# Score products from stacked q parts and doubled k parts, in both mixers of an encoder trunk

## The chip, the core and the metric

The kernel runs on one core of a Trainium2 chip. The metric is the device time of one execution in microseconds. Several executions of one program are timed, and their median is compared. One execution is also profiled: a trace of the instructions of each engine and of the DMAs, and a page that sums it up. The engines are called PE (matrix products; PEld is its loading of the stationary operand), DVE (vector), ACT (scalar and activation), POOL (general purpose, and one of the issuers of DMAs) and SP (issuer of DMAs).

## The reference

Two requests, 512 and 256 tokens of width 1024, go through a trunk of two layers with shared weights. Each layer is a half-weighted SwiGLU, a mixer, and another half-weighted SwiGLU. The first mixer has a gated part and a windowed attention with 8 query heads on 2 key heads; the second is a neighbourhood attention with 16 heads on a grid 64 wide. Only the scores matter for the change, and in both mixers they are a product over the 64 elements of a head:

```python
# first mixer (windowed attention, HEAD_DIM = 64)
s = jnp.einsum('bnqgrd,bnkgd->bngrqk', qb, kw).astype(jnp.float32) * (HEAD_DIM ** -0.5)
...
# second mixer (neighbourhood attention)
s = jnp.einsum('bchd,bacjhd->bhcaj', q_row, k_win).astype(jnp.float32) * (HEAD_DIM ** -0.5)
```

All is float32 in the reference. After the scores come a bias or mask, a softmax and a product with the values.

## The kernel before

**Parts.** Activations lie with the features on the 128 partitions and the tokens (512 of the prompt, then 256 of the sample, 768 in all) along the free dimension. PE multiplies operands of type float32r. To keep accuracy, each operand is split into a high part (a rounding cast on ACT) and a low part (the rest, a subtraction on DVE). A product of two split operands is then the sum of three products: high with high, high with low, low with high. `mm3` (L235) does this for the projections.

**Scores.** A projection of 128 output features gives two heads: head 0 in partitions 0 to 63 and head 1 in 64 to 127. `parts2` splits such a block of q or k for both heads at once, with the factor −1/8 for q. `halves3` makes the scores of both heads for one block of 128 queries: three products, and for each of them one matmul per head, whose operands are 64 partitions high. So a block takes six matmuls of half height, the two heads alternating. Their results go to PSUM banks of the pool `aux`, which has four.

**First mixer (`mixer0`).** k is projected once, for both key heads, and v with it. Then come four projections of q (`q_heads`), each for two of the eight query heads; q tiles have four buffers. `attention` runs as a chain beside the other projections: `score` for a pair of q projections and a block of queries, `turn` (transposes of the probabilities and their split) and `values`.

**Second mixer (`mixer1`).** Eight pairs of heads follow each other. `qk(pr)` loads the weights and projects q and k of a pair, for the prompt columns first and then for the sample columns, four projections; DVE scales each result by the row norm into a tile `qk`. The prompt tokens are kept turned: tile columns are shifted by 64 against the token order, and to have blocks of queries that wrap around, the tile is 64 columns longer (`TE`), with its first 64 columns copied to its end (L1709). The chain `parts(pr)` then splits them into the tiles of q and k, appends the pair to `heads`, and ends. The q and k tiles have one buffer each, so `parts(pr)` waits until the scores of the pair before are placed. The chain `attention` takes the pairs in order: while there is no new pair in `heads` it looks again every 0.5; then it places `scores(pr, 0)` and `scores(pr, 1)` (prompt, two blocks of queries each) and `scores(pr, 2)` (sample, two blocks), with the transposes and value products of the pair before in between. `bias` makes the additive terms for the next pair on POOL.

**What sets the order.** PE executes its instructions in the order in which the Python code emits them. The other engines' order is chosen by a scheduler from the dependencies. The emission is a hand-made interleaving: `self.t` is a clock that advances with each emitted matmul by an estimate (`mmul`: columns/2400, at least 0.107, in us). Chains are generators that yield a delay and are stepped by `tick` after every `mm3` when the clock has reached their time. `run_until` and `drain` step chains without emitting anything else, and set the clock forward to each chain's time while doing so. In `mixer1` this is the loop over quads of heads:

```python
for qd in range(4):
    for i in (0, 1):
        if last:
            self.drain(last)
        new = qk(2 * qd + i)
        ...
        last = self.spawn(parts(2 * qd + i, new, vt, 2 * i))
        if i == 0:
            v_heads(qd, vt)
```

So `parts` of an even pair runs beside the projections of v (`v_heads`), and `parts` of an odd pair is drained at once, before the next pair's `qk`, or, for the last pair, before the output projection.

Of the kernel before, what the change touches and what calls it, by code (L numbers as in the profile page):

```python
# [10 lines left out]
F32 = mybir.dt.float32  # L11
F32R = mybir.dt.float32r
# [40 lines left out]
class Trunk:  # L53
# [1051 lines left out]
    def norm_r(self, mp, cols):  # L1105
# [4 lines left out]
        if cols:  # L1110
            acc = mp.tile([P, T], F32, tag="accp", name="accp")
            for a, b, to in self.turned():
                nc.scalar.copy(acc[:, to : to + b - a], self.acc[:, a:b])
            yield 1.0
# [115 lines left out]
    def halves3(self, ps, st, mv):  # L1230

        for i, (a, b) in enumerate(((0, 0), (0, 1), (1, 0))):
            for h in (0, 1):
                self.mmul(ps[h], st[h][a], mv[h][b], i == 0, i == 2)
# [14 lines left out]
    def mixer0(self):  # L1249
# [54 lines left out]
        kh = mp.tile([P, T], F32R, tag="kh", name="kh")  # L1304
        kl = mp.tile([P, T], F32R, tag="kl", name="kl")
# [13 lines left out]
        for g in (0, 1):  # L1319
            c0, c1 = GROUPS[g]  # L1320
            t = roped(pkv[g][0], c0, c1)
            self.parts2(kh[:, c0:c1], kl[:, c0:c1], t)
# [8 lines left out]
        def q_heads(m):  # L1331
            q = [mp.tile([P, T], F32R, tag=f"q{n}", name=f"q{n}", bufs=4) for n in "hl"]
            w = self.unit("l0_w_in", 0, KD, 1024 + m * P, P)
            for g in (0, 1):
                c0, c1 = GROUPS[g]
                t = roped(self.proj(w, xs, GROUPS[g]), c0, c1)
                self.parts2(q[0][:, c0:c1], q[1][:, c0:c1], t, -0.125)
            qheads.append(q)

        def score(rp, n):  # L1340
# [4 lines left out]
            rows = lambda h: slice(h * 64, h * 64 + 64)  # L1345
            mv = [(kh[rows(h), cols], kl[rows(h), cols]) for h in (0, 1)]
# [6 lines left out]
            for r in (0, 1):  # L1353
# [4 lines left out]
                q = qheads[2 * rp + r]  # L1358
                self.halves3(dst, [tuple(t[rows(h), n * P : (n + 1) * P] for t in q) for h in (0, 1)], mv)
# [155 lines left out]
    def mixer1(self):  # L1515
# [6 lines left out]
        TE = TA + 64  # L1522
# [25 lines left out]
        SCORE = [(128 * j + 64, 128 * j + 64 * (j == 0), 128 * j + 256 - 64 * (j == 3), 64 * (j == 0)) for j in range(4)]  # L1548
        SCORE += [(TE + P * j, TE + 96 * j, TE + 96 * j + 160, 96 * j) for j in range(2)]
# [10 lines left out]
        def scores(pr, s):  # L1560
# [3 lines left out]
            for i in (0, 1):  # L1564
# [5 lines left out]
                rows = lambda h: slice(h * 64, h * 64 + 64)  # L1570
                self.halves3(
                    dst, [tuple(t[rows(h), qc : qc + P] for t in q) for h in (0, 1)],
                    [tuple(t[rows(h), c0:c1] for t in k) for h in (0, 1)],
                )
# [109 lines left out]
        def parts(pr, t, vt, hv):  # L1684
# [4 lines left out]
            q, k = ([mp.tile([P, TE + TB], F32R, tag=f"{n}{i}", name=f"{n}{i}") for i in "hl"] for n in "qk")  # L1689
            st = mp.tile([P, 4, 16], F32, tag="st", name="st", bufs=2)  # L1690
            for g, (c0, c1) in enumerate(((0, TE), (TE, TE + TB))):
                for which, d in ((0, q), (1, k)):
# [257 lines left out]
```

## Time and profile before

| | |
|---|---|
| median of 3 runs | 2551.85 us (2550.28 to 2552.0) |
| profiled execution, its own time | 2551.05 us |
| its span, first to last instruction | 2549.3 us |
| mean granted PE clock | 0.998 |
| first score product of the first mixer | at 540.1 us of the span |
| score products of the second mixer | begin from 1731.6 to 1984.4 us of the span |

The span is shorter than the execution's time by what lies before the first and after the last instruction. Busy times are unions of the instructions' durations. Matmuls overlap in the pipeline, so the time that one takes from the engine is read from one start to the next and not from its duration. A group of instructions is named by its line, engine, operation and tiles as output<-inputs; the products of one helper all bear the helper's line, L192, and are told apart by their tiles: `kh`, `kl`, `qh` and `ql` are the high and low parts of k and q before. The granted clock is the share of full speed that PE's throttle let through.

### The profile page before, as it was taken

How to read it: one execution, taken by the hardware profiler on the slowest of the kernel's cores; microseconds unless marked ns; L12 is line 12 of the kernel's file. 1: busy time of each engine (PE TensorE's matmuls, PEld its weight loads, DVE VectorE, ACT ScalarE, POOL GpSimd, SP SyncE). 2: the span in 40 equal slices, each digit the busy share in tenths (PEclk: the TensorE clock that was granted, in tenths of full speed). 3: DMA queues.
4: the chain of work that ended last, by engine and by line, in shares of the span. 5: the costliest groups of instructions: out<-in, count | busy, mean ns of one | idle time of the engine just before them, and what ended most of it. 6: DMA issues, size and time to landing. Idle time of an engine off the chain costs nothing.

```text
span 2549.3 us, 42552 instructions
## 1 busy us (share of the span) xinstructions
PE 2532.7 (99%) x15160; PEld 2460.6 (97%) x15160; DVE 2092.9 (82%) x4199; ACT 1369.1 (54%) x2843; POOL 323.3 (13%) x398
## 2 busy tenths in 40 slices
PE   9999999999999999999999999999999999999998
PEld 9999999988899999999999999998999899999998
DVE  8987888888879778788988888886667598878887
ACT  7544455556665545445655445554555475444553
POOL 1110110000111111110111011112112111101100
PEclk9999999999999999999999999999999999999999
DMA  8654555431256445552665455532222256545541
GB/s 238 159 132 121 131 134 147 147 96 61 77 140 177 115 130 125 131 130 82 155 154 133 119 128 125 120 127 69 65 61 77 76 150 168 131 119 125 124 125 53
DMA packets 187156, 310.88 MB, mean 122 GB/s; under 512 B 31680, under 2 KB 46528, under 8 KB 186944
## 3 DMA queue, kind: packets, MB, share of 16 engines
q1 hardware_dynamic: 149248, 240.49, 29.3%
q0 software_dynamic: 36864, 67.13, 16.7%
q8 instruction: 119, 1.95, 0.3%
q14 instruction: 93, 0.76, 0.1%
q10 hardware_dynamic: 832, 0.55, 0.1%
HBM read 298.65 MB, written 15.07 MB: 123 GB/s over the span
## 4 chain that ended last, share of the span: by engine, by line
PE 92%; DVE 4%; ACT 1%; issue 1%; DMA 1%; POOL 0%; SPq 0%; ACTq 0%; DVEq 0%; POOLq 0%
PE ps_mm L192 60%; PE ps_aux L192 30%; PE ps_aux L203 1%; DVE wlo L169 1%; DMA s<-in_w 1%; DMA raw<-in_w 0%; DVE u L588 0%; DVE s L746 0%; ACT whi L168 0%; DVE tl L256 0%; ACT p L1217 0%; ACT ug L1493 0%; DMA x<-in_x 0%; DVE db L256 0%; DVE o L1402 0%
## 5 line engine op out<-in xcount | busy, mean ns | idle before, releaser
L168 ACT CAST whi<-s 128x512 fp32r<-128x512 f32 x508 | 310.6, 620 | 384.2 <-PE ps_mm L192 199.1
L169 DVE TENSOR_TENSOR wlo<-s,whi 128x512 fp32r<-128x512 f32 x508 | 344.8, 686 | 173.6 <-ACT whi L168 152.4
L149 POOL DMA_DIRECT2D s<-in_w x256 | 223.8, 917 | 1439.9 <-DVE db L256 376.4
L168 ACT CAST whi<-rawp 128x512 fp32r<-128x512 f32 x344 | 211.5, 619 | 255.1 <-issue 100.0
L169 DVE TENSOR_TENSOR wlo<-rawp,whi 128x512 fp32r<-128x512 f32 x344 | 234.0, 685 | 23.2 <-ACT whi L168 14.2
L192 PE MATMUL ps_mm<-db,whi 128*128 128x384 f32 (+1 forms) x948 | 240.2, 334 | 0.0
L192 PE MATMUL ps_aux<-dt,whi 128*128 128x384 f32 x880 | 223.3, 334 | 0.0
L192 PEld LDWEIGHTS ps_mm<-db,whi 128*128 128x128 f32 x948 | 170.9, 188 | 0.0
L192 PE MATMUL ps_mm<-db,wlo 128*128 128x384 f32 (+1 forms) x474 | 158.3, 334 | 0.8 <-DVE wlo L169 0.8
L192 PEld LDWEIGHTS ps_aux<-dt,whi 128*128 128x128 f32 x880 | 158.9, 188 | 0.0
L192 PE MATMUL ps_aux<-dt,wlo 128*128 128x384 f32 x440 | 147.2, 334 | 0.4 <-DVE wlo L169 0.3
L168 ACT CAST whi<-raw 128x512 fp32r<-128x512 f32 x164 | 100.4, 619 | 67.8 <-PE ps_mm L192 44.3
L169 DVE TENSOR_TENSOR wlo<-raw,whi 128x512 fp32r<-128x512 f32 x146 | 99.0, 687 | 20.8 <-ACT whi L168 19.8
L588 DVE TENSOR_TENSOR u<-ps_aux,u 128x384 f32<-128x384 f32 x176 | 97.0, 551 | 7.6 <-PE ps_aux L192 7.6
L1217 ACT ACTIVATE p<-p,st 128x256 f32<-128x256 f32 (+3 forms) x144 | 69.1, 481 | 50.5 <-DVE st L1212 50.4
L192 PEld LDWEIGHTS ps_mm<-db,wlo 128*128 128x128 f32 x474 | 89.0, 188 | 1.4 <-DVE wlo L169 1.4
L582 ACT COPY u<-ps_mm 128x384 f32<-128x384 f32 x176 | 83.4, 474 | 1.9 <-PE ps_mm L192 1.6
L192 PEld LDWEIGHTS ps_aux<-dt,wlo 128*128 128x128 f32 x440 | 82.6, 188 | 1.0 <-DVE wlo L169 1.0
L746 DVE TENSOR_TENSOR s<-s,rawp 128x512 f32<-128x512 f32 x120 | 81.8, 687 | 2.0
L598 ACT ACTIVATE u<-u 128x384 f32<-128x384 f32 x88 | 46.2, 525 | 67.2 <-DVE u L597 67.1
L746 DVE TENSOR_TENSOR s<-rawp,s 128x512 f32<-128x512 f32 x120 | 81.8, 682 | 0.1
L192 PE MATMUL ps_aux<-dn,whi 128*128 128x384 f32 x320 | 81.2, 334 | 0.0
(772 smaller groups left out, 8231.2 us busy)
## 6 DMA issues: line engine op xcount, KB each, us to landing
rawp<-in_w SPq DMA_DIRECT2D x384, 256.0 KB, 3.1
s<-in_w SPq DMA_DIRECT2D x256, 256.0 KB, 2.8
s<-in_w POOLq DMA_DIRECT2D x256, 256.0 KB, 4.9
raw<-in_w SPq DMA_DIRECT2D x163, 256.0 KB, 2.8
xdm<-x SPq DMA_DIRECT2D x16, 384.0 KB, 2.3
x<-in_x SPq DMA_DIRECT2D x16, 192.0 KB, 4.5
x<-xdm SPq DMA_DIRECT2D x8, 384.0 KB, 4.9
tab<-skew SPq DMA_DIRECT2D x8, 256.0 KB, 3.7
```

The costliest lines, as they stand in the source:

```text
L149: self.nc.gpsimd.dma_start(f, y, accum_op=ALU.add)
L168: i = nc.scalar.copy(hi, src).ins
L169: self.behind = i, (eng or nc.gpsimd).tensor_tensor(out=lo, in0=src, in1=hi.bitcast(F32), op=ALU.subtract).ins
L192: self.nc.tensor.matmul(out, lhsT=lhsT, rhs=rhs, start=start, stop=stop, **kw)
L203: self.nc.tensor.transpose(out, src, self.ident)
L582: nc.scalar.copy(e[n, out], bank[key, n])
L588: nc.vector.tensor_tensor(out=t, in0=bank[key, n], in1=t, op=ALU.add)
L598: nc.scalar.activation(t, t, AF.Silu, scale=-1.0 if i else 1.0)
L746: f = lambda o, x, y: self.nc.vector.tensor_tensor(out=o, in0=x, in1=y, op=ALU.add)
L1217: nc.scalar.activation(outs[i - n0], outs[i - n0], AF.Exp, scale=-1.0, bias=mn[:, i : i + 1], accum_out=sm[:, i : i + 1])
```

## The change

Both mixers store the parts of q and k in another way, so that one product over 128 partitions covers two of the part products.

- **q stacked** (`stacked`). There is one q tile per head. In the head's own 64 partitions lies the high part, and in the other 64 the low part. Each is written by an op on 64 partitions (ACT for the high part, DVE for the low part).
- **k in both row halves** (`twice`). There are, per head, a tile (or half of a tile) with the high part of k in both row halves, and one with its low part in both.
- **Two products per head** (`stacks`). q stacked times k high twice, and times k low twice, both of full height: (high + low) · high + (high + low) · low. Low with low, which was left out before, is now in the sum. A block of queries takes four matmuls instead of six.
- **First mixer.** `twice` writes both row halves on ACT and DVE: four ops of 64 partitions on each, where there was one of 128. q tiles have three buffers instead of four.
- **Second mixer.** `twice` writes the head's own half only (`both=False`), k before q, and when both column groups are written, a DMA issued by POOL for each head copies the parts to the other half: 64 partitions of 2 × 768 elements. A delay of 2.0 on the emission clock is added before the pair is appended to `heads`.
- **No wrap copy.** The scaling into `qk` now writes the prompt columns in turned order, in two ops, so the copy of L1709 and the 64 extra columns are gone, and the blocks of queries start at multiples of 128.
- The turned copy of the norm's sums takes the tile `k0` instead of one of its own.

```diff
+    def stacks(self, ps, st, mv):
+        for h in (0, 1):
+            for i in (0, 1):
+                self.mmul(ps[h], st[h], mv[h][i], i == 0, i == 1)
+
+    def stacked(self, out, src, h, scale):
+        a, b = (slice(i * 64, i * 64 + 64) for i in (h, 1 - h))
+        self.nc.scalar.activation(out[a], src[a], AF.Copy, scale=scale)
+        self.nc.vector.scalar_tensor_tensor(
+            out=out[b], in0=src[a], scalar=scale, in1=out[a].bitcast(F32), op0=ALU.mult, op1=ALU.subtract
+        )
+
+    def twice(self, hi, lo, src, h, both=True):
+        a, b = (slice(i * 64, i * 64 + 64) for i in (h, 1 - h))
+        for r in (a, b) if both else (a,):
+            self.nc.scalar.copy(hi[r], src[a])
+        for r in (a, b) if both else (a,):
+            self.nc.vector.tensor_tensor(out=lo[r], in0=src[a], in1=hi[a].bitcast(F32), op=ALU.subtract)
...
@@ first mixer
-        kh = mp.tile([P, T], F32R, tag="kh", name="kh")
-        kl = mp.tile([P, T], F32R, tag="kl", name="kl")
+        ks = [[mp.tile([P, T], F32R, tag=f"k{n}{h}", name=f"k{n}{h}") for n in "hl"] for h in (0, 1)]
...
-            self.parts2(kh[:, c0:c1], kl[:, c0:c1], t)
+            for h in (0, 1):
+                self.twice(*(u[:, c0:c1] for u in ks[h]), t, h)
...
-            q = [mp.tile([P, T], F32R, tag=f"q{n}", name=f"q{n}", bufs=4) for n in "hl"]
+            q = [mp.tile([P, T], F32R, tag=f"q{h}", name=f"q{h}", bufs=3) for h in (0, 1)]
...
-                self.parts2(q[0][:, c0:c1], q[1][:, c0:c1], t, -0.125)
+                for h in (0, 1):
+                    self.stacked(q[h][:, c0:c1], t, h, -0.125)
...
@@ second mixer, parts
-            q, k = ([mp.tile([P, TE + TB], F32R, tag=f"{n}{i}", name=f"{n}{i}") for i in "hl"] for n in "qk")
+            q = [mp.tile([P, T], F32R, tag=f"q{h}", name=f"q{h}") for h in (0, 1)]
+            k = [mp.tile([P, 2, T], F32R, tag=f"k{h}", name=f"k{h}") for h in (0, 1)]
             st = mp.tile([P, 4, 16], F32, tag="st", name="st", bufs=2)
-            for g, (c0, c1) in enumerate(((0, TE), (TE, TE + TB))):
-                for which, d in ((0, q), (1, k)):
-                    self.parts2(d[0][:, c0:c1], d[1][:, c0:c1], t[g, which], None if which else -0.125)
+            for which in (1, 0):
+                for g, (c0, c1) in enumerate(GROUPS):
+                    for h in (0, 1):
+                        if which:
+                            self.twice(*(k[h][:, i, c0:c1] for i in (0, 1)), t[g, 1], h, False)
+                        else:
+                            self.stacked(q[h][:, c0:c1], t[g, 0], h, -0.125)
                     yield 0.3
+                for h in (0, 1) if which else ():
+                    a, b = (slice(i * 64, i * 64 + 64) for i in (h, 1 - h))
+                    nc.gpsimd.dma_start(k[h][b], k[h][a])
+            yield 2.0
             heads.append((q, k, st, vt, hv))
...
@@ second mixer, qk
-                    res[g, which] = t = mp.tile([P, n if g else TE], F32, tag=f"qk{g}", name=f"qk{g}", bufs=2)
-                    nc.vector.tensor_tensor(out=t[:, :n], in0=ps[:, :n], in1=self.rt[:, t0:t1], op=ALU.mult)
-                    if g == 0:
-                        nc.vector.tensor_copy(t[:, TA:TE], t[:, 0 : TE - TA])
+                    res[g, which] = t = mp.tile([P, n], F32, tag=f"qk{g}", name=f"qk{g}", bufs=2)
+                    for a, b, to in ((0, n, 0),) if g else ((64, TA, 0), (0, 64, TA - 64)):
+                        nc.vector.tensor_tensor(
+                            out=t[:, to : to + b - a], in0=ps[:, a:b], in1=self.rt[:, t0 + a : t0 + b], op=ALU.mult
+                        )
```

In both mixers the calls of `halves3` become calls of `stacks`, with a whole q tile of each head as stationary operand and the two k parts of that head as moving ones.

More of the change, by code (lines that the diff above doesn't have):

```diff
@@ L1110, in norm_r @@
         if cols:
-            acc = mp.tile([P, T], F32, tag="accp", name="accp")
+            acc = mp.tile([P, 2, T], F32, tag="k0", name="accp")[:, 0, :]
             for a, b, to in self.turned():
@@ L1228, in finish_rows @@
             )
[L1230 to L1234, printed above, removed]
+    def stacks(self, ps, st, mv):
[14 more added lines that the diff above has]
+            self.nc.vector.tensor_tensor(out=lo[r], in0=src[a], in1=hi[a].bitcast(F32), op=ALU.subtract)
     def parts2(self, hi, lo, src, scale=None):
@@ L1344, in score @@
             cols = slice(blks[0] * P, (blks[-1] + 1) * P)
-            rows = lambda h: slice(h * 64, h * 64 + 64)
-            mv = [(kh[rows(h), cols], kl[rows(h), cols]) for h in (0, 1)]
+            mv = [[t[:, cols] for t in k] for k in ks]
             m0 = (blks[0] - n + 1) * P
@@ L1357, in score @@
                 dst = [t[:, o : o + nk * P] for t in ps]
-                q = qheads[2 * rp + r]
-                self.halves3(dst, [tuple(t[rows(h), n * P : (n + 1) * P] for t in q) for h in (0, 1)], mv)
+                self.stacks(dst, [t[:, n * P : (n + 1) * P] for t in qheads[2 * rp + r]], mv)
                 todo += dst
@@ L1521, in mixer1 @@
         self.xcols = lambda k, c0, c1: tuple(self.cut(t[k], c0, c1) for t in xs)
-        TE = TA + 64
         mb = mp.tile([P, NMASK], BF16, tag="mb", name="mb")
@@ L1546, in mixer1 @@
         ot = {}
-        SCORE = [(128 * j + 64, 128 * j + 64 * (j == 0), 128 * j + 256 - 64 * (j == 3), 64 * (j == 0)) for j in range(4)]
-        SCORE += [(TE + P * j, TE + 96 * j, TE + 96 * j + 160, 96 * j) for j in range(2)]
+        SCORE = [(P * j, max(P * j - 64, 0), min(P * j + 192, TA), 64 * (j == 0)) for j in range(4)]
+        SCORE += [(TA + P * j, TA + 96 * j, TA + 96 * j + 160, 96 * j) for j in range(2)]
         pp = {}
@@ L1569, in scores @@
                 dst = [t[:, o : o + n] for t in ps]
[L1570 to L1574, printed above, removed]
+                self.stacks(dst, [t[:, qc : qc + P] for t in q], [[t[:, i, c0:c1] for i in (0, 1)] for t in k])
                 ps_list += dst
```

## The prediction

> **What bounds the kernel now.** I read the page's engine shares first, then the chain that ended last, then the busy time by stretch for the two mixers, and last the timeline around the score products.
>
> ```profile
> span 2549.3 us, 42552 instructions
> PE   2532.7 (99%) x15160; PEld 2460.6 (97%) x15160; DVE 2092.9 (82%) x4199; ACT 1369.1 (54%) x2843; POOL 323.3 (13%) x398
> PE 92%; DVE 4%; ACT 1%; issue 1%; DMA 1%; POOL 0%; SPq 0%; ACTq 0%; DVEq 0%; POOLq 0%
> ...
> 500.00:680.00 180.00, 177.96 (x1102) 152.56 (x1101) 151.37 (x415) 110.60 (x231) 9.25 (x8) 0.99 0.27 85
> 1720.00:2000.00 280.00, 279.97 (x2061) 253.80 (x2061) 193.11 (x554) 148.15 (x389) 58.31 (x82) 1.00 0.22 70
> ```
>
> In the last two rows the columns are stretch, length, and busy time of PE, PEld, DVE, ACT and POOL. PE is the bound. In the second mixer's score stretch (1720 to 2000) it was busy 279.97 of 280 us, so each PE step saved there is time saved, and each new PE wait is time lost. In the first mixer (500 to 680) it stood 2.0 us, and DVE was 84% busy.
>
> **Removed: half-height score products.** A timeline row is start, duration, engine, line, output<-inputs, shape.
>
> ```profile
> 1800.72 0.28 PE L192 MATMUL ps_mm<-wlo,xh3a 128*128 128x256 f32 x1
> 1800.84 0.28 PE L192 MATMUL ps_mm<-whi,xl3a 128*128 128x256 f32 x1
> 1801.05 0.39 PE L192 MATMUL ps_aux<-kh,qh 64*128 64x256 f32 x2
> 1801.27 0.28 PE L192 MATMUL ps_aux<-kl,qh 64*128 64x256 f32 x2
> ...
> 1801.60 0.28 PE L192 MATMUL ps_aux<-kl,qh 64*128 64x192 f32 x2
> 1801.71 0.28 PE L192 MATMUL ps_aux<-kh,ql 64*128 64x192 f32 x2
> 1801.92 0.39 PE L192 MATMUL ps_mm<-whi,xh4a 128*128 128x256 f32 x1
> 1802.14 0.28 PE L192 MATMUL ps_mm<-wlo,xh4a 128*128 128x256 f32 x1
> 1802.26 0.28 PE L192 MATMUL ps_mm<-whi,xl4a 128*128 128x256 f32 x1
> ...
> 552.04 0.39 PE L192 MATMUL ps_mm<-whi,xl3a 128*128 128x512 f32 x1
> ...
> 553.41 0.40 PE L192 MATMUL ps_mm<-wlo,xh3a 128*128 128x512 f32 x1
> 553.65 0.40 PE L192 MATMUL ps_mm<-whi,xl3a 128*128 128x512 f32 x1
> ...
> L192 PE MATMUL ps_aux<-kh,qh x144: 247/340/686, 540.1 to 1984.3; 64*128 64x256 f32 x64, 64*128 64x192 f32 x32, 64*128 64x160 f32 x32, 64*128 64x384 f32 x16
> ```
>
> Durations overlap, so I count from start to start. Plain products of 256 columns follow each other at 0.12 us. The two heads' half-height products (x2) start together, so six take three slots; but going into a group costs 0.21 instead of 0.12, and coming out 0.21 and 0.22. From 1800.84 to 1802.14 are 1.30 us; without two plain steps the group costs 1.06. The new group is eight full-height products without a change of height: four at 0.12 and four of 192 columns at 0.11 (the narrow pairs' step), 0.92. It saves about 0.15. A 384-column group: 1.37 us less two steps of 0.235 is 0.90; four products at 0.176 (0.235 × 384/512) are 0.70; it saves 0.20.
>
> The counts give the groups. The x144 are 72 pairs; the second mixer has 24 groups of two pairs, the first mixer 8 of two and 8 single ones of 384. So 24 × 0.15 = 3.6 us in the second mixer, 8 × 0.15 + 8 × 0.20 = 2.8 in the first: **6.4 us** of PE.
>
> **Given back in the first mixer.**
>
> ```profile
> 654.94 0.44 PE L192 MATMUL ps_aux<-kh,qh 64*128 64x384 f32 x1 [1.71 <-DVE tl L256]
> 655.44:658.85 3.41, 3.41 (x15) 2.29 (x12) 3.41 (x10) 3.38 (x7) 1.27 (x1) 0.50 0.03 7
> ```
>
> Here PE waits for a bank that DVE empties late. By then PE would be 11 groups (about 2 us) earlier and DVE no earlier: most of that becomes a longer wait. I count 1.8 us back (bounds 0 and 3), so the first mixer gains 1.0. More DVE and ACT work falls here (k copied four times instead of once, q twice), before 540 and near 620, ahead of products that come microseconds later; if that cover is gone, the last q column part adds one op, 0.4 us. With three q buffers instead of four, the fourth q pair waits for the first pair's last scores, which ran at 609; q was written from 616.
>
> **Added on ACT and DVE in the second mixer.**
>
> ```profile
> L1240 ACT CAST kh<-qk 128x256 fp32r<-128x256 f32 x8 | 3.2, 406 | 3.4 <-DVE qk L1707 3.4
> L1241 DVE TENSOR_TENSOR kl<-qk,kh 128x256 fp32r<-128x256 f32 x8 | 3.3, 416 | 0.0
> L1625 DVE TENSOR_TENSOR o<-ps_aux,tb 64x256 f32<-64x256 f32 x16 | 6.7, 417 | 4.6 <-ACT tb L1624 4.4
> ```
>
> 64 rows cost what 128 do (417 against 416 ns), so splitting an op by heads doubles it: about 2 us more DVE and ACT work in each of eight pairs, some 16 us, less two small copies per pair. DVE has 87 us free in the stretch, so I count nothing except where k is late.
>
> **Added: a transfer between k and the first score.** The new k parts fill one row half per head; POOL transfers copy them, all 768 columns, to the other half. They can start only after the parts of the sample columns, which come from the last projection of the pair. Before, the first score of a pair read prompt columns only, ready long before. Now it waits for last projection, scaling, two splits, and transfer. Behind the waiting product PE's whole queue stands, next pair's projections or v's included.
>
> ```profile
> 1765.91 0.28 PE L192 MATMUL ps_mm<-xh,wlo 128*128 128x256 f32 x1
> ...
> 1766.82 0.36 PE L192 MATMUL ps_aux<-kh,qh 64*128 64x192 f32 x2
> ...
> 1767.41 0.42 DVE L1241 TENSOR_TENSOR kl<-qk,kh 128x256 fp32r<-128x256 f32 x1
> ...
> 1792.98 0.42 DVE L1241 TENSOR_TENSOR kl<-qk,kh 128x256 fp32r<-128x256 f32 x1
> ...
> 1794.01 0.36 PE L192 MATMUL ps_aux<-kh,qh 64*128 64x192 f32 x2
> ...
> 1969.56 0.36 PE L192 MATMUL ps_aux<-kh,qh 64*128 64x192 f32 x2
> ...
> 1972.55 0.41 DVE L1241 TENSOR_TENSOR kl<-qk,kh 128x256 fp32r<-128x256 f32 x1
> ...
> s<-in_w SPq DMA_DIRECT2D x256, 256.0 KB, 2.8
> s<-in_w POOLq DMA_DIRECT2D x256, 256.0 KB, 4.9
> xdm<-x SPq DMA_DIRECT2D x16, 384.0 KB, 2.3
> x<-xdm SPq DMA_DIRECT2D x8, 384.0 KB, 4.9
> ...
> L149 POOL DMA_DIRECT2D s<-in_w x256 | 223.8, 917 | 1439.9 <-DVE db L256 376.4
> ```
>
> The transfers carry 384 KB each (64 rows × 2 × 768 × 4 bytes). No SBUF-to-SBUF one is in the trace. Transfers of that size land 2.3 to 4.9 us after issue; POOL's, which also add, take 2.1 longer than SP's of the same size, and POOL's issue alone is 0.92. So between 2.9 (2.3 and two thirds of that issue, since SP issues too) and 7.0 (4.9 and 2.1); I take **4.0**, nearer the undisturbed 2.3, and the second 0.9 behind the first, a POOL issue later. POOL itself is free there: its bias sums for a pair come before the pair's scores of necessity.
>
> *Odd pairs.* `drain` runs the emission clock past the pair's parts without placing any PE work, so the first score stays 0.9 us behind the last projection product (1765.91, 1766.82) whatever the new 2.0 delay says. k's last split ends at 1767.83; I let head 0's end there and head 1's an op later. Head 0's copy lands at 1767.9 + 4.0 = 1771.9, head 1's at 1772.8. PE waits 5.1 us, runs two products (0.2), waits 0.7 more: 5.8. Pairs 1, 3 and 5 stand alike in the code; pair 7 has DVE work of the output stage in front: 1972.96 + 0.1 + 4.0 is 7.5 after 1969.56, with head 1 8.2. Sum 3 × 5.8 + 8.2 = **25.6 us**.
>
> *Even pairs* have v's projections as cover, and there the delay works: 2.0 on the emission clock, which counts 0.107 for a 0.12 product, is 2.2 us of PE. Pair 2: score at 1796.2, first landing 1793.4 + 0.1 + 4.0 = 1797.5, wait 1.3, and 0.7 for head 1: 2.0. Taking pair 0 like it, 4 × 2.0 = **8.0 us**.
>
> *Clock.* After the wait of 1.71 us at 654.94 PE's granted clock was 0.50 for 3.41 us: 1.7 us lost. I add 1.7 for each odd pair (bounds 0.9 and 2.6, by how much of the slow time falls into the wait or a second 3.41 follows) and half of it for each even one: 6.8 + 3.4 = **10.2 us**. The Trainium skill ("TensorE: Matmul & The Clock Gate", What's actually happening) has the clock halve only after an idle window of about 3.4 us; by that the even pairs would lose nothing more and the sum would be 3.4 smaller. The trace disagrees: 1.71 us was enough.
>
> **Sum**: 25.6 + 8.0 + 10.2 − 3.6 − 1.0 = +39.2. The profiled execution took 2551.05 us (span 2549.3 and 1.75 around it), 0.8 under the median 2551.85 of the three runs. 2551.05 + 39.2 = 2590.2; I forecast **2590**.
>
> **Rivals.**
> - *The transfer is covered* (other side: faster). If the first score came 6 us or more behind the last projection, only the gain would be left: 2551 − 4.6 to − 6.4, about **2545.5**. For it: the new delay, and PE's clean record here. Against: 0.9 us on odd pairs, a shift of 4.3 at most on even ones. 9%, a third of that within 0.2%.
> - *A quick transfer.* At 2.9 an odd wait is 4.7 (pair 7: 7.1), an even one 0.9, clock 0.9 per odd pair: 21.2 + 3.6 + 3.6 − 4.6 = +23.8, **2575**; with k's splits also a microsecond earlier about 2566. For: the 2.3 row. 15%.
> - *DVE or ACT becomes the bound*: were the doubled 16 us to show where k and banks are late, half of it would: **2598**. For: DVE at 84% in the first mixer. Against: 87 us free in the second. 8%.
> - *Full height costs PE more.* If leaving the half height saved none of the gaps, a fourth slot per set would be added: 48 × 0.115 + 16 × 0.12 + 8 × 0.176 = 8.8 slower instead of 6.4 faster; with the waits 2604, without them 2560. The gaps of 0.21 speak against it. 4%. The Trainium skill (same page, Part 3) says that small products in different row groups run at once and gain by it; by that rule alone this change loses. The trace agrees on the pairs, and shows what switching costs.
> - The change not doing what it says is no case of its own: the counts below would tell.
>
> **How the numbers follow.** The main case has 64%. Its own range: landing 2.9 to 7.0 with the clock's bounds spans 2573 to about 2621, of which the end at 7.0, POOL's adding transfers, is the less likely. The range is **2564 to 2615**: it holds nearly all of the main case and of the quick, DVE and full-height rivals, and leaves out the covered one. About 0.2% (5 us) is what a measurement can tell from no change. Faster 0.06, same 0.04, slower 0.90.
>
> **What would show it.** Score products 288 at 128 rows instead of 432 at 64, with no 0.21 gaps: step one. PE waits in 1720 to 2000, ended by DMA into k, eight times two, odd pairs near 5 us: step two. Granted clock 0.50 for 3.4 us behind them: step three. PE busy near 280 of 280 there, and no wait on k, would make me wrong; so would a landing under 2 us, or scores placed after the next pair's first projections.

## The result, and the profile after

The changed kernel takes **2624.48 us** (median of 4 runs, 2623.50 to 2626.96), against 2551.15 us of the kernel before in the same session (4 runs): a ratio of 1.0288, interval 1.0276 to 1.0300. It is slower, by 73.3 us where 39.2 were forecast, and outside the range of 2564 to 2615. Times and ratios here and below leave out one execution, of 3601.36 us at a granted clock of 0.65, of the kernel without a transfer.

The page of the changed kernel, engine shares and granted clock by slices, and its waits of PE from 1680 us on (engine, tile, line <- what ended the wait: us in total, times, longest):

```profile
span 2622.2 us, 42418 instructions
PE 2547.3 (97%) x15016; PEld 2482.7 (95%) x15016; DVE 2121.9 (81%) x4245; ACT 1388.6 (53%) x2887; POOL 331.5 (13%) x414
...
PEclk9999999999999999999999999998989899999999
```

```profile
PE ps_aux L192 <- DMA k<-k: 55.8, 16, 13.0
```

The span is 72.9 us longer. PE's busy time is *up* by 14.6 us, although it ran 144 instructions fewer: matmuls at half clock count as busy for longer (one of 256 columns for 0.41 us at 1817.25, for 0.28 at full clock). So the shares of the page would mislead here. The waits say more: 16 of them, two for each of the eight pairs, all ended by the transfer of k. Before, the same view had no wait on k at all.

Busy time of the changed kernel in one stretch (stretch, length, busy us of PE, PEld, DVE, ACT, POOL, then granted clock, DMA share, GB/s). This is the score stretch that the prediction quoted at 279.97 of 280:

```profile
1720.00:2000.00 280.00, 238.56 (x1595) 221.47 (x1594) 167.50 (x472) 128.63 (x335) 54.19 (x85) 0.90 0.24 70
```

PE got through 1595 matmuls there instead of 2061, stood for 41.4 us, and ran at 0.90 of its clock. Standing and slow clock together make the loss.

**The waits, one by one**: the timeline of PE in the changed kernel, one row per pair and wait (the bracket is the idle time ahead of it and what ended it); pairs 0 (its second, of 0.69, left out), 1, 2 and 7:

```profile
1735.40 0.74 PE L192 MATMUL ps_aux<-k,q 128*128 128x192 f32 x2 [2.84 <-DMA k<-k]
...
1776.85 0.71 PE L192 MATMUL ps_aux<-k,q 128*128 128x192 f32 x2 [5.93 <-DMA k<-k]
1778.57 0.71 PE L192 MATMUL ps_aux<-k,q 128*128 128x192 f32 x2 [1.00 <-DMA k<-k]
1813.21 0.61 PE L192 MATMUL ps_aux<-k,q 128*128 128x192 f32 x2 [3.47 <-DMA k<-k]
1815.83 0.98 PE L192 MATMUL ps_aux<-k,q 128*128 128x192 f32 x3 [2.01 <-DMA k<-k]
...
2038.62 0.71 PE L192 MATMUL ps_aux<-k,q 128*128 128x192 f32 x2 [13.00 <-DMA k<-k]
2040.69 0.53 PE L192 MATMUL ps_aux<-k,q 128*128 128x192 f32 x1 [1.35 <-DMA k<-k]
```

Pairs 3 and 5 are like pair 1 (5.91 and 1.07; 6.09 and 0.91), pairs 4 and 6 like pair 2 (3.51 and 2.27; 3.55 and 2.19). From start to start, less a plain step at the clock of the place, the two waits of a pair cost 7.3 to 7.4 us in pairs 1, 3 and 5, 14.7 in pair 7 (36.7 for the odd ones), 3.9 in pair 0 and 5.8 to 6.1 in pairs 2, 4 and 6 (21.9). That is 58.6 us for the 16 waits, some 0.2 more for each than its idle time.

**The clock behind them**: stretches of the changed kernel, columns as above. I chose their borders at the changes of the clock:

```profile
1734.81:1741.64 6.83, 5.55 (x24) 5.31 (x25) 1.43 (x8) 2.33 (x9) 1.28 (x2) 0.50 0.09 26
1775.77:1782.60 6.83, 4.74 (x15) 3.98 (x16) 1.67 (x10) 1.97 (x8) 1.28 (x2) 0.50 0.21 55
1857.69:1867.93 10.24, 5.65 (x17) 4.69 (x18) 2.57 (x13) 1.97 (x8) 1.78 (x3) 0.50 0.37 101
...
2028.36:2045.43 17.07, 5.46 (x16) 4.57 (x17) 4.60 (x19) 2.78 (x10) 1.06 (x2) 0.50 0.72 200
```

Every pair is followed by slow time: five times 6.83 us, twice 10.24, once 17.07, 71.7 us in all. 32.5 of it fall into the waits, counted from the start of the product before, where they cost nothing more; the other 39.2 cost half, **19.6 us**.

**Why the landing is late**: the tile k of the changed kernel, its transfers and their time from issue to landing, and the DMA shares of three stretches around transfers:

```profile
L192 PE MATMUL ps_aux<-k,q x192: 234/278/529, 1735.4 to 2057.8; 128*128 128x192 f32 x64, 128*128 128x256 f32 x64, 128*128 128x160 f32 x64
...
L1712 POOL DMA_DIRECT2D k<-k x16: 509/540/632, 1730.9 to 2031.0; - x16
...
DMA to landing us min/median/max: 3.5/5.2/9.6
```

```profile
1772.00:1779.00 7.00, 1.14 (x4) 0.96 (x5) 0.55 (x2) 0.07 (x1) 1.06 (x2) 0.77 0.66 186
1809.00:1816.00 7.00, 1.52 (x10) 1.14 (x9) 1.95 (x5) 0.15 (x1) 1.06 (x2) 0.81 0.61 150
2030.00:2041.00 11.00, 1.02 (x3) 0.82 (x4) 0.60 (x2) 0.00 (x0) 1.06 (x2) 0.50 0.98 257
```

In pair 7 the DMA engines are 98% busy (the x tiles and weights of the next stage are on their way as well), and the two landings take 8.0 and 9.6 us; that the load is what holds them up is read from this row, and no run takes it away. In the other pairs the first lands 3.5 to 4.4 us after its issue and the second, issued 0.5 to 0.8 later, 5.1 to 5.7 after its own.

**What leads up to the transfer**, pair 2: timeline of the changed kernel.

```profile
1805.21 1.40 DVE L1240 SCALAR_TENSOR_TENSOR q<-qk,q 64x512 fp32r<-64x512 f32 x2
...
1806.64 0.69 DVE L1635 TENSOR_TENSOR o<-ps_aux,tb 64x512 f32<-64x512 f32 x1
...
1807.36 0.42 DVE L1727 TENSOR_TENSOR qk<-ps_mm,rt 128x256 f32<-128x256 f32 x1
...
1808.16 0.41 DVE L1635 TENSOR_TENSOR o<-ps_aux,tb 64x256 f32<-64x256 f32 x1
...
1808.60 0.87 DVE L1250 TENSOR_TENSOR k<-qk,k 64x256 fp32r<-64x256 f32 x2
...
1809.55 1.20 POOL L1712 DMA_DIRECT2D k<-k  x2 [10.29 <-issue]
```

PE was done with this pair's last k projection at about 1804.2 (its last product starts at 1803.95). DVE took it up at 1807.36: it was still at the doubled q splits of the prompt columns and at the outputs `o` of the pair before. The transfer goes out at 1809.55, when PE has just reached the scores (its last product ahead of them starts at 1809.46). So the cover that the even pairs have was used up by DVE before the transfer began.

### The profile page after: what moved, and what is told of

The parts are those of the page before. It is cut to its first block, busy times and chain, and to the rows that moved or that the text cites. A ratio compares the mean times of both kernels' runs of the same rounds, so it can differ in the third digit from the quotient of the medians.

```text
span 2622.2 us, 42418 instructions
## 1 busy us (share of the span) xinstructions
PE 2547.3 (97%) x15016; PEld 2482.7 (95%) x15016; DVE 2121.9 (81%) x4245; ACT 1388.6 (53%) x2887; POOL 331.5 (13%) x414
## 5 line engine op out<-in xcount | busy, mean ns | idle before, releaser
L192 PE MATMUL ps_aux<-k,q 128*128 128x192 f32 (+2 forms) x192 | 34.8, 327 | 55.8 <-DMA k<-k 55.8
L192 PEld LDWEIGHTS ps_aux<-k,q 128*128 128x128 f32 x192 | 30.9, 232 | 60.3 <-issue 54.2
L1212 DVE CUSTOM_DVE_ANT_0 p<-ps_aux,add 128x256 f32<-128x256 f32 (+2 forms) x96 | 30.4, 365 | 68.4 <-PE ps_aux L192 68.0
```

The costliest lines, as they stand in the source:

```text
L192: self.nc.tensor.matmul(out, lhsT=lhsT, rhs=rhs, start=start, stop=stop, **kw)
L1212: nc.vector.tensor_tensor_reduce(out=outs[i - n0], in0=ps_list[i - n0], in1=adds[i - n0], scale=1.0, scalar=init[i - n0], op0=ALU.add, op1 ...
```

## The experiments

All kernels are the changed one with the edit shown, and all ratios are to the kernel before.

| kernel | us | ratio (95% interval) |
|---|---|---|
| first mixer alone | 2549.43 | 0.9994 (0.9985 to 1.0003) |
| no transfer, k written twice | 2552.02 | 1.0004 (0.9995 to 1.0013) |
| transfer by column group | 2560.31 | 1.0037 (1.0023 to 1.0050) |
| delay of 6.0 | 2600.49 | 1.0195 (1.0181 to 1.0209) |
| late drain, whole transfer | 2587.72 | 1.0142 (1.0128 to 1.0155) |
| late drain, transfer by column group | 2559.83 | 1.0034 (1.0022 to 1.0047) |
| late drain, no transfer | 2569.01 | 1.0070 (1.0058 to 1.0083) |
| transfer as plain float32 | 2626.64 | one run |
| no transfer, parts in the old order | 2550.71 | 0.9999 (0.9991 to 1.0008) |
| transfer by column group, k projected first | 2554.59 | 1.0016 (1.0007 to 1.0025) |
| whole transfer, k projected first | 2602.22 | 1.0198 (1.0184 to 1.0212) |
| waits filled with products | 2613.14 | 1.0245 (1.0231 to 1.0259) |
| no transfer, low copy on ACT | 2549.69 | 0.9993 (0.9984 to 1.0002) |
| one transfer instead of two | 2613.65 | 1.0241 (1.0226 to 1.0257) |

### Which half of the change costs

The first mixer of the changed kernel with the second mixer of before (its `parts`, `qk` and blocks of queries too):

```diff
-                self.stacks(dst, [t[:, qc : qc + P] for t in q], [[t[:, i, c0:c1] for i in (0, 1)] for t in k])
+                self.halves3(
+                    dst, [tuple(t[rows(h), qc : qc + P] for t in q) for h in (0, 1)],
+                    [tuple(t[rows(h), c0:c1] for t in k) for h in (0, 1)],
+                )
...
-                            self.twice(*(k[h][:, i, c0:c1] for i in (0, 1)), t[g, 1], h, False)
...
+                    self.parts2(d[0][:, c0:c1], d[1][:, c0:c1], t[g, which], None if which else -0.125)
```

> Only the first mixer is changed; the second is as before. Theory (the loss is PE waiting for the k transfers of the second mixer, and its slow clock behind those waits; the full-height products themselves gain): the first mixer gains the 2.1 to 2.4 us by which a product at 2120.0/808.1 us of the trace of before stood 2.1 us earlier at 806.0 in the changed kernel: about 2549 us against 2551.2. Rival (the doubled ACT and DVE work makes the rest of the change slow too): 2552 us or more.

2549.43 us, and none of the waits on k. The first mixer costs nothing; its own stretch is 2.3 us shorter in the profile, which the ratio alone can't tell from no change. All of the loss is the second mixer's.

Then the second mixer without the transfer, k's other row half written by ACT and DVE as in the first:

```diff
-                            self.twice(*(k[h][:, i, c0:c1] for i in (0, 1)), t[g, 1], h, False)
+                            self.twice(*(k[h][:, i, c0:c1] for i in (0, 1)), t[g, 1], h)
...
-                for h in (0, 1) if which else ():
-                    a, b = (slice(i * 64, i * 64 + 64) for i in (h, 1 - h))
-                    nc.gpsimd.dma_start(k[h][b], k[h][a])
```

> The second mixer's k is doubled by ACT and DVE ops, as in the first mixer, and no DMA is issued; all else as in the changed kernel. Theory (transfers): no wait on k is left, since the first score reads prompt columns that are split before the last projection ends; PE keeps 3.2 us of the second mixer and 2.4 of the first: about 2546 us. Rival (DVE is the bound that was missed: it gets 16 us more work on top of the changed kernel's): half of this shows as PE waits, 2555 to 2562 us, and PE waits stand behind DVE.

2552.02 us: the 73 us hang on the transfer. But the time lies between the two expectations, and nothing that can be measured is left of PE's gain. Waits of PE in this kernel from 1680 on:

```profile
PE ps_aux L192 <- DVE q L1240: 3.1, 3, 1.0
```

These are new, and on DVE, and so are 0.8 on `st` and 0.6 on `tl`: q's parts now come last.

### What makes the wait long

First, the place of the scores:

```diff
-            yield 2.0
+            yield 6.0
```

> The delay before a pair is appended is 6.0 instead of 2.0. Theory (the delay is covered by v's projections on even pairs and by nothing on odd ones): even pairs' waits fall from 5.8 us (3.9 for the first pair) to under 1.5, odd pairs' stay at 7.4 and the last pair's at 14.7; waits 56 down to about 40, with the clock 2624 down to 2594 us. Rival (the delay does nothing, since DVE and the transfer move along with PE): 2624 us. Second rival (the delay works on all pairs): below 2575 us.

2600.49 us, where 2594 were expected. Waits on k fall to 41.7 us (11 instead of 16). The even pairs keep only a second wait of 1.6 to 1.7 us, and pair 0 has none. The odd pairs are where they were, pair 1 for one (PE timeline of this kernel):

```profile
1770.21 0.72 PE L192 MATMUL ps_aux<-k,q 128*128 128x192 f32 x2 [5.97 <-DMA k<-k]
```

So `drain` does take the delay's effect away there, as the prediction read it.

Second, the size of the transfer: each column group goes as soon as it is written, and only the 256 sample columns are left for the end.

```diff
+                    for h in (0, 1) if which else ():
+                        a, b = (slice(i * 64, i * 64 + 64) for i in (h, 1 - h))
+                        nc.gpsimd.dma_start(k[h][b, :, c0:c1], k[h][a, :, c0:c1])
                     yield 0.3
-                for h in (0, 1) if which else ():
-                    a, b = (slice(i * 64, i * 64 + 64) for i in (h, 1 - h))
-                    nc.gpsimd.dma_start(k[h][b], k[h][a])
```

> Four transfers a pair instead of two: per head one for the prompt columns, issued when these are split, and one for the sample columns. Theory (the first score waits because the transfer holds the sample columns, which come last): odd pairs' waits fall from 7.4 us to 0 to 2, even ones' from 5.8 to 0 to 2.5; with the clock 2548 to 2568 us, likeliest 2556. Rival (a transfer costs PE its time whatever columns it holds, by landing 4 to 5 us after issue under DVE's backlog): 2600 us or more.

2560.31 us, with a sixth of the waits. Its DMA issues (KB each, median us to landing) and waits:

```profile
k<-k POOLq DMA_DIRECT2D x16, 256.0 KB, 3.2
...
k<-k POOLq DMA_DIRECT2D x16, 128.0 KB, 3.0
```

```profile
PE ps_aux L192 <- DMA k<-k: 9.3, 5, 2.6
```

The first score of a pair reads prompt columns only, so it now waits for the earlier piece alone; in pair 1 head 0's has landed in time and head 1's, the second of the two, has not. The landing itself gets shorter by less than the bytes: at the least it takes 2.3 us for 128 KB (issued at 1796.85) and 2.9 for 256 KB (at 1793.34), against 3.5 for 384 KB in the changed kernel, and pair 1's second one of 256 KB takes 5.2 as before. What the split saves is mostly the wait for the sample columns: in pair 1 head 0's prompt columns go out at 1762.0, where the whole went at 1772.7.

Third, whether the second transfer holds up the first. Head 0 by transfer, head 1 written by ACT and DVE:

```diff
-                            self.twice(*(k[h][:, i, c0:c1] for i in (0, 1)), t[g, 1], h, False)
+                            self.twice(*(k[h][:, i, c0:c1] for i in (0, 1)), t[g, 1], h, h == 1)
...
-                for h in (0, 1) if which else ():
+                for h in (0,) if which else ():
```

> Head 0's k parts still go to the other row half by a transfer, head 1's are written there by ACT and DVE. In the changed kernel head 0's landing takes 3.5 to 4.4 us from issue and head 1's 5.1 to 5.7, outside pair 7. Theory (the two transfers share the DMA engines): alone, head 0's lands in 2.9 to 3.3, so odd first waits fall from 6.4 to about 5.5 and even ones from 3.8 to about 3.0; no second wait; 2592 to 2602. Rival (the landing of one transfer is a price of its own, whatever runs beside it): 3.5 to 4.4 stays, first waits stay at 6.4 and 3.8, only the second waits (14.5 in all) go; 2605 to 2612.

2613.65 us. That the two share the DMA engines falls as the cause of the first landing: alone, the transfer is no faster. Landing of the eight transfers, and the first wait of pair 1:

```profile
DMA to landing us min/median/max: 3.5/4.6/10.0
```

```profile
1778.17 2.04 PE L192 MATMUL ps_aux<-k,q 128*128 128x192 f32 x8 [7.41 <-DMA k<-k]
```

It is 3.5 us in pair 2 as with two, and 4.8 in pair 1 against 4.1; why it is longer there stays open. Its issue is later as well, at 1773.25 instead of 1772.66, with head 1's extra parts on DVE. With one transfer the odd pairs wait once for as long as they waited twice, and the time is above both expectations. Transfers issued by another engine than POOL were not tried.

Last, the same transfers with both sides declared float32, since float32r might have meant a conversion:

```diff
-                    nc.gpsimd.dma_start(k[h][b], k[h][a])
+                    nc.gpsimd.dma_start(k[h][b].bitcast(F32), k[h][a].bitcast(F32))
```

> The same two transfers a pair from POOL, but read and written as float32 instead of float32r, bit for bit the same. If the conversion from float32r to float32r slows the packets (6144 bytes took 425 ns where 3072 bytes of a plain transfer took 121), packets fall to about 240 ns, the second landing comes about 0.7 us earlier, waits on k fall from 56 to about 47 us and the time to about 2610. If the packets' time is that of two transfers that share the DMA engines, nothing changes: 2624 us.

2626.64 us in one execution, with 55.6 us of waits on k: no difference.

### What the slow clock costs

Ahead of the first score of each pair, products of constants that nobody reads: 12, 15, 26 or 58 of them by pair, to keep PE busy through the wait.

```diff
+                    self.warm(58 if pr == 7 else 26 if pr % 2 else 15 if pr else 12)
                     scores(pr, 0)
```

> The changed kernel, with products of constants placed in front of the first score of each pair, about as many as fill the first wait (12, 26, 15, 26, 15, 26, 15, 58 of 512 columns, 0.22 us each); they leave the output alone. Theory (behind the waits PE runs at half clock, 19.6 us in all): the clock stays up but for the second waits, 2624 down to 2605 to 2612 us. Rival (the slow clock costs nothing, since the engines catch up in that time): 2622 us or more.

2613.14 us, 11.3 less and 1 above the expected range, with 193 products *more*. The places of two of the stretches above, in this kernel:

```profile
1734.80:1741.60 6.80, 5.78 (x41) 5.23 (x39) 1.33 (x8) 2.24 (x9) 1.30 (x2) 1.00 0.32 83
...
2030.30:2037.00 6.70, 5.52 (x17) 4.55 (x18) 2.68 (x13) 1.97 (x8) 0.00 (x0) 0.50 0.07 20
```

The slow time of the second mixer goes from 71.7 to 13.7 us, and its cost outside the waits from 19.6 to 5.9. That is 13.7 less, of which 11.3 arrive; the fill takes some of it. So the idle time, and not the score products, brings the slow clock, and its size is about right.

### Moving k earlier, or the scores later

`drain` of each pair's parts after the next pair's first projection instead of before it, and of the last pair's beside the output projection, with the whole transfer, the split one, and none:

```diff
-        def qk(pr):
+        def qk(pr, before):
...
+                    if before:
+                        self.drain(before)
+                        before = None
...
-                if last:
-                    self.drain(last)
-                new = qk(2 * qd + i)
+                new = qk(2 * qd + i, last)
...
-        self.drain(last)
-        self.run_until(lambda: len(done) >= KD - 2)
+        self.run_until(lambda: len(done) >= KD - 2 and KD - 1 in ot)
```

> The changed kernel with its transfers as they are, but each pair's parts are drained only after the next pair's first projection is placed (24 products of 512 columns, 5.5 us of PE), and the last pair's run beside the output projection. Theory (odd pairs wait because nothing is placed between their last projection and their first score): the odd pairs' first wait falls from 6.1 us to between 0.5 and 2, the second wait of 1.2 stays, the last pair's 14.7 falls below 11; even pairs as before at 5.8. With the clock 2624 down to 2585 to 2600 us. Rival (the wait moves along, since DVE and the transfers are slowed by the added cover): 2615 us or more.

> Both: four transfers a pair, by column group, and the later drain. Theory: no wait on k is left on odd pairs; on even ones at most 0.4 (first pair); PE keeps its gain of both mixers, 2545.5 to 2548 us. Rival (transfers and DVE's extra work cost PE in other places): 2552 us or more.

> k doubled by ACT and DVE ops, no transfer, and the later drain. Theory (what the run without transfers gave back, 5.4 us of waits behind the q parts on odd pairs and the last pair, is again the missing cover): those waits go, 2545.5 to 2548 us. Rival (DVE is too full for 16 us more): 2551 us or more.

2587.72, 2559.83 and 2569.01 us; the last two missed. The waits on k go as meant (17.9 us with the whole transfer, 0.8 with the split one), but others come. Waits of PE with the split transfer, and where the longest stands:

```profile
PE ps_aux L192 <- DVE tl L256: 7.1, 6, 2.0
```

```profile
1798.10 0.58 PE L192 MATMUL ps_aux<-tl,vt 128*128 128x256 f32 x1 [1.97 <-DVE tl L256]
```

The stretch around it (columns as in the stretches above) is at half clock:

```profile
1797.48:1804.30 6.82, 6.20 (x29) 6.20 (x30) 4.38 (x13) 1.65 (x6) 0.75 (x2) 0.50 0.12 38
```

Now the value products wait for the turned probabilities' low parts. The order of the code gives a reason: `attention` lags behind the projections, `parts` of the next pair waits until the scores are placed, and then `drain` places turning and values with no projections between them. Without any transfer this is worse (12.9 us in 9 waits), so it is not the transfer's doing. It was not tried with another order of `attention`.

Then k before q in the projections of a pair, with the split and the whole transfer:

```diff
-                for which in (0, 1):
+                for which in (1, 0):
                     ps = todo.pop(0)[2] if todo else self.proj(ws[which], xs, GROUPS[g])
```

> Four transfers a pair by column group, and k projected before q in each group. Theory (what is left with four transfers, 9.3 us of waits on odd pairs and 3.4 of clock, is the time from the prompt columns' k projection to the landing): that projection now ends 5.4 us earlier, no wait on k is left, 2560 down to 2546 to 2549 us. Rival (the 16 us more of DVE work is what the transfers hide): waits behind DVE appear, 2552 us or more.

> Two transfers a pair as in the changed kernel, but k projected before q. The last k projection now ends 2.8 us earlier (24 products of 256 columns). Theory (the wait is the path from the last k projection through split and transfer to the first score): the first wait falls by 2.8 us on each pair, odd 6.1 to 3.3, even 3.6 to 0.8, last 13.2 to 10; second waits stay; waits 56 down to 34, and with a third of the clock loss gone 2624 down to about 2595 us. Rival (the transfers wait for something else, POOL or the DMA engines): 2615 us or more.

2554.59 us, on the rival's side, and 2602.22, 7 above the expected 2595. With the split transfer **no wait on k is left**: it is covered. The time is still 0.16% above the kernel before. Waits of PE, two of the seven on `wlo` in its timeline, and the stretch behind the first of them:

```profile
PE ps_mm L192 <- DVE wlo L169: 3.8, 7, 1.2
PE ps_aux L203 <- DVE st L1212: 1.0, 1, 1.0
```

```profile
1711.12 0.80 PE L192 MATMUL ps_mm<-xh0a,wlo 128*128 128x512 f32 x1 [1.16 <-DVE wlo L169]
1817.34 0.50 PE L192 MATMUL ps_mm<-xh0a,wlo 128*128 128x512 f32 x1 [0.55 <-DVE wlo L169]
```

```profile
1711.13:1714.54 3.41, 3.41 (x8) 2.73 (x9) 3.41 (x8) 2.06 (x6) 0.92 (x1) 0.50 0.77 255
```

`wlo` is the low part of a weight, and the products that wait are among the first of a k projection. `qk` loads and splits q's weights ahead of k's, and k's are now needed first. So these waits come with the new order of the projections and not with the extra copies: the whole transfer in this order has the same ones (0.48 for `whi`, 1.17, and three of 0.54 to 0.56), and no kernel in the old order has them. They begin ahead of any score. The stretch from the end of the first mixer to the first scores, between the products that start at 808.11 and 1725.11 before, is 3.7 us longer, nearly all of it the waits of 0.48 and 1.16 there and the half clock behind them (1.7). From there to the output projection (its first product starts at 2012.50 before) it takes 288.1 us against 287.4: the gain of the second mixer's score products is given back by 3.0 us of waits, three of 0.55 on `wlo`, 1.0 on `st` and 0.4 on `tl`. The first mixer keeps its 2.4. Splitting k's weights first was not tried. With the whole transfer the waits on k are 35.4 us: half a pair's projection is not enough cover for it.

### What eats the gain without a transfer

The kernel without the transfer, with q ahead of k by column group as before the change:

```diff
-            for which in (1, 0):
-                for g, (c0, c1) in enumerate(GROUPS):
+            for g, (c0, c1) in enumerate(GROUPS):
+                for which in (0, 1):
```

> No transfer, and q and k parts in the order of the kernel before (prompt columns of q and k, then sample columns). Theory (the run without transfers waited on even pairs 1.1 us behind q parts, because k parts of both column groups were put in front of them): these waits go, 2552 down to 2546 to 2549 us. Rival (DVE's doubled work sets the waits, in whatever order): 2551 us or more.

2550.71 us: the waits on q are gone, others on DVE have come (`tl` 2.4, `st` 0.8). The gain did not appear, a miss. The first mixer keeps its part: between the products that start at 538.6 and 808.1 before, 269.5 us apart, it takes 267.1 to 267.2 us here, without a transfer above and in the next kernel. The second mixer, from the product at 1725.11 before to the output projection, takes 290.1 without a transfer above, 288.9 here and 287.9 in the next kernel, against 287.4. Last, the same with the low part's second copy on ACT:

```diff
-        for r in (a, b) if both else (a,):
+        for r in (a, b) if both and not act else (a,):
             self.nc.vector.tensor_tensor(out=lo[r], in0=src[a], in1=hi[a].bitcast(F32), op=ALU.subtract)
+        if act:
+            self.nc.scalar.copy(lo[b], lo[a].bitcast(F32))
```

> The kernel of the run without transfers and with q before k by column group (2550.7), but the second row half of k's low part is copied by ACT from the first instead of being subtracted by DVE: four DVE ops of 0.42 us less in each pair, some 13 us of DVE's 363 in 1680 to 2130, four ACT ops of 0.4 more. Theory (DVE's extra ops ate the gain): PE's waits on DVE there (4.1 on tl, 0.8 on st) fall to 1 or less, 2546.5 to 2549. Rival (what eats it is the chain of splits, whoever runs it): waits of about the same length remain or pass to ACT, 2550 to 2552. Neither has a wait on k longer than 1 us.

2549.69 us, between the two expectations. Busy time in 1680 to 2130 with the low copies on DVE, and on ACT:

```profile
1680.00:2130.00 450.00, 444.91 (x2940) 417.71 (x2939) 363.12 (x884) 278.44 (x663) 84.90 (x113) 1.00 0.33 97
```

```profile
1680.00:2130.00 450.00, 446.29 (x2946) 419.86 (x2946) 346.47 (x853) 293.19 (x696) 84.65 (x114) 1.00 0.34 97
```

and the waits of the kernel with ACT's copies:

```profile
PE ps_mm L192 <- ACT whi L168: 1.8, 2, 1.5
```

DVE is 16.7 us freer, and the waits on `tl` and `st` are gone. In their place PE waits 1.5 us for ACT and 0.6 for POOL, once each, in the last pair, and half clock follows for 3.41 us. So the waits move to the engine that makes the copies. This shows DVE's share in the waits; in time the two kernels can't be told apart. Neither this kernel nor the first mixer alone can be told from the kernel before: both intervals reach past 1. None of the tried kernels beats it measurably.

## Why the prediction failed, point by point

| term, us | forecast | measured |
|---|---|---|
| score products, second mixer | −3.6 | −3.1 |
| first mixer | −1.0 | −2.4 |
| odd pairs' waits | +25.6 | +36.7 |
| even pairs' waits | +8.0 | +21.9 |
| slow clock | +10.2 | +19.6 |
| sum | +39.2 | +72.7 |

The span grew by 72.9, so the measured terms account for all but 0.2. How the loss is shared between the waits and the clock is less sure: with the idle times alone taken as the waits, the clock's share is 20.9. The first mixer's is counted between the same two products on either side of it, 334.5 and 332.1 us apart.

**Score products: right.** 288 of full height instead of 432: 192 on the tile k, above, and 96 in the first mixer. A group of the changed kernel on its timeline:

```profile
1824.73 0.28 PE L192 MATMUL ps_mm<-whi,xl3a 128*128 128x256 f32 x1
1824.85 1.07 PE L192 MATMUL ps_aux<-k,q 128*128 128x256 f32 x8
1825.76 0.30 PE L192 MATMUL ps_mm<-whi,xh4a 128*128 128x256 f32 x1
1825.90 0.28 PE L192 MATMUL ps_mm<-wlo,xh4a 128*128 128x256 f32 x1
```

From 1824.73 to 1825.90 are 1.17 us, against 1.30 before; the gaps of 0.21 are gone. That is 0.13 for each of 24 groups, where 0.15 were taken.

**First mixer: right in its parts, one missed.** Its waits grew by 1.5 us (3.0 to 4.5), where 1.8 were taken. But the longest (a row of the changed kernel's timeline, idle in brackets) became a little shorter than the 1.71 of before, and the clock stayed full in the stretch behind it:

```profile
656.01 0.44 PE L192 MATMUL ps_aux<-kh,q 128*128 128x384 f32 x1 [1.41 <-DVE tl L256]
```

```profile
655.40:658.90 3.50, 2.32 (x10) 1.71 (x11) 3.37 (x6) 2.62 (x6) 1.47 (x1) 1.00 0.15 55
```

That saved the 1.7 us that the slow clock cost there before. It is luck: in two kernels with the same first mixer, those with filled waits and with float32 transfers, the clock is at 0.50 for 3.41 us there, from 658.08 and 658.38. In the second of them the first mixer takes 268.6 us from the product at 538.6 before to that at 808.1, where the changed kernel takes 267.1.

**The transfer as the bound: right.** Sixteen waits, two for each pair, odd ones independent of the delay.

**The step "I take 4.0, and the second 0.9 behind the first": mis-sized.** 4.0 stands for the first landing outside pair 7 (3.5 to 4.4). The second comes 1.4 to 2.7 us behind the first, so that the second waits are 13.0 us in all instead of 5.6, and in pair 7 the landings take 8.0 and 9.6, beyond the end of 7.0 that the prediction allowed. The prediction counted DVE's work near pair 7, and not what the DMA engines carry there: they are 98% busy.

**The step "DVE has 87 us free in the stretch, so I count nothing except where k is late": this is the one that failed.** On the even pairs it is late. The prediction let head 0's last split end 2.7 us ahead of the score's place (1793.5 and 1796.2); in pair 2 it ended 0.6 ahead, 2.1 later. With half a microsecond from there to POOL's issue, the wait was 3.47 instead of 1.3. On the odd pairs the split came some 0.3 later and the issue 0.5 after it: 5.93 instead of 5.1. Free time as a sum over 280 us says nothing of the order in DVE's queue, where k's splits stand behind the doubled q splits and the outputs. All first waits together are 17.6 us longer than forecast: about 10 of it because k's first split ends later against the score's place, 3.4 by the first landings (pair 7 alone 4.0), and the rest on the way from split to issue and from landing to score. So this step is the largest single one in the waits, and not the whole miss. In the three kernels without a transfer and with `drain` where it was, DVE, ACT or POOL are late in other places: 2.1 to 4.8 us of new waits, and 1.7 of half clock in one of them, use up the second mixer's gain of 3.1.

**The step "1.7 for each odd pair and half of it for each even one": half of what came.** The slow time was taken as one stretch of 3.41 us for each pair. There were two in a row for every even pair, and two, three or five for the odd ones. The kernel with filled waits bears the size out. On the Trainium skill's rule ("TensorE: Matmul & The Clock Gate", What's actually happening), that the clock halves only after an idle window of about 3.4 us, the first waits of pairs 1 to 7 (3.47 to 13.0) would all qualify; but 2.84 in pair 0 was enough too, and in the kernel with split transfers 2.41 and 2.60 were.

**The rivals.** A covered transfer was to give 2545.5. The kernel with k first and split transfers has it covered, and takes 2554.59: its gain is given back partly by late splits of k's weights, which come with that order, and partly by waits on DVE among the scores. No kernel reached 2545.5. DVE as the bound (8% with 2598) was kept apart from the main case, where it is part of it: its lateness adds to the transfer. A quick transfer of 2.9 did not come, the shortest landing was 3.5. That full height costs PE more is refuted by the group above, 0.13 us shorter.

## What to carry over

A transfer between two engines' steps is a chain, and its price is the whole chain from the last producer to the first consumer: queue ahead of the split, split, issue, landing, each read from the timeline at that place, with the DMA engines' load in that window and not the median of a quiet stretch. An engine with free time on average can still be late where it counts; look at what stands in its queue ahead of the one op that is waited for. Before trading PE work for copies, compare the gain (here 5.5 us) with what one wait of 3 us costs: the wait, and then some microseconds of half clock.

## What the runs showed of the hardware that was not expected

- **The landing of a transfer within the chip has a large part that does not follow its size**: at the least 2.3 us for 128 KB and 2.9 for 256 KB (transfers by column group), 3.5 for 384 KB. From these three an estimate is 0.6 us for each 128 KB on top of 1.7. A second one issued 0.5 to 0.8 us behind lands 1.4 to 2.7 us behind.
- **The slow clock comes in steps of 3.41 us**: 3.41, 6.83, 10.24 and 17.07 in the runs here.
- **Its onset is no matter of the wait's length alone.** In the kernel with split transfers two waits of nearly one length, and the stretches behind them:

```profile
1767.98 0.93 PE L192 MATMUL ps_aux<-k,q 128*128 128x192 f32 x6 [2.32 <-DMA k<-k]
1837.50 1.01 PE L192 MATMUL ps_aux<-k,q 128*128 128x192 f32 x5 [2.41 <-DMA k<-k]
```

```profile
1768.00:1771.40 3.40, 3.40 (x20) 2.98 (x21) 1.51 (x9) 1.97 (x8) 1.33 (x3) 1.00 0.60 154
...
1838.00:1841.40 3.40, 3.40 (x11) 2.82 (x10) 1.95 (x11) 1.97 (x8) 1.29 (x2) 0.50 0.36 68
```

2.32 us of idle time left the clock alone and 2.41 halved it, while a wait of 1.5 us in the kernel with ACT's copies, with one of 0.6 behind it, halved it too. That fits windows of 3.41 us at fixed times, in which the idle share decides. No run here set out to show it, but the traces bear it out. In the changed kernel the slow stretches shown start 40.96, 122.88 and 293.55 us behind the first one at 1734.81, which is 12, 36 and 86 steps of 3.4133. In the kernel with late drain and split transfers the same two waits for `tl`, 0.41 and 1.97 (once 1.96), come three times. Half clock follows at 1797.48 and 1940.84, and not in between:

```profile
1870.62 0.38 PE L192 MATMUL ps_aux<-tl,vt 128*128 128x256 f32 x1 [1.97 <-DVE tl L256]
```

```profile
1870.70:1874.10 3.40, 3.40 (x29) 3.40 (x30) 2.94 (x8) 0.94 (x3) 0.05 (x1) 1.00 0.16 40
```

There an edge of the windows, 21 steps behind 1797.48 at 1869.16, cuts the longer wait into 0.5 and 1.5. Counted in such windows between 500 and 2200 us of every trace, full clock with 1.9 us or more of idle time in a window was always followed by half clock, and with less than 1.4 never.
